# Three quarters of the V sums kept in PSUM, and the experts' stage written as a fixed pipeline in program order

## The chip, the cores and the metric

The kernel runs on 1 core of one Trainium2 chip. The metric is device time in microseconds, the median of several runs of the whole kernel; lower is better. A profile is one such execution with the hardware profiler on. PE is TensorE (PEld its weight loads), DVE is VectorE, ACT is ScalarE, POOL is GpSimd and SP is SyncE, which here issues the ordinary DMAs.

## The reference

One encoder layer on 256 tokens of width 2048 in float32: a retention and a recurrent group in parallel, cross attention over 256 memory tokens, then a feed-forward layer of 16384 one-neuron experts, and a last RMSNorm. The change is in the experts' layer:

```python
def peer_ffn(xn, w_q, sub_keys, u_tab, v_tab):
    q = (xt @ w_q).reshape(t, PEER_HEADS, 2, PEER_HALF)
    sub_scores = jnp.einsum('thcd,hckd->thck', q, sub_keys)
    ...                      # eid: 8 heads x top 16 experts of each token; gate: their softmax
    u = u_tab[eb]
    act = jax.nn.gelu(jnp.einsum('td,tkd->tk', xb, u))
    return jnp.einsum('tk,tkd->td', gb * act, v_tab[eb])
```

## The kernel before

The 16384 experts are split. 104 of 128 columns of them (`RD`) are computed **densely**, for all 256 tokens, in 13 chunks (`NCH`) of 8 columns of 128 experts. The experts of the other 24 columns are **gathered** row by row for the tokens that chose them, and a few that don't fit in the gathers' 28 slots per token tile (`BASE`) go through a short "spill" path.

A dense chunk has two halves. The U half (`u_chunk`, L909) multiplies the tokens by 8 blocks of U: each block is two loads of 512 KB, and each load is one **step** of 8 matmuls with `hi` and 8 with `lo`. The V half (`v_unit`, L935) multiplies the gated activations by V: four column groups `dc` of 512 columns, four steps `q` each, and 12 matmuls per step (two token tiles, two k, three products). So a half chunk is 16 steps either way.

Every step has the same preparation. SP loads 512 KB into one of 4 `raw` buffers (`raw_tile`, L105). `split` (L110) rounds it on ACT to `hi` (L114, 4 buffers) and has DVE subtract to get `lo` (L115, 3 buffers), which frees `raw`. PE then multiplies (U: L124 with `hi`, L127 with `lo`; V: L931 to L933). Every second step of U ends a block: ACT copies a half of the sum (L917), DVE adds it (L918), ACT takes the gelu (L919). After each `dc` group of V, DVE adds the two finished PSUM tiles into the output rows `hh` (L951), 8 times per chunk.

Between the halves stands `prep` (L878): two loads of gate values `gd` into `raw` buffers, two DVE multiplies (L883) and the split of the gated activations into `ah` and `al` (L894, L895; chunks 8 to 11 use a second place, `xe`).

The gathers run beside all this. `chosen` (L991) makes 112 tasks: POOL gathers 128 rows (L964) into a ring of four `gat` buffers, three tasks ahead; DVE then either takes their dot products with the tokens (`dot`, L981, whose product goes to a PSUM tile `junk` that nobody reads) or adds them weighted into `hh` (`axpy`, L989). `weigh` (L975) finds up to 8 weights before a block of dots. A task costs 2.2 credits, a weight 0.225, and every step pays in 0.9 (`RC`, `Weave.pump`), so a task falls to about every 2.4 steps.

The program is written in the order of chunks: six U halves first (`LEAD`), then V of chunk i and U of chunk i+6 in turn until U is done (7 pairs), then V alone (chunks 7 to 11), then `v_final` with chunk 12 and the output. But the order in which each engine gets its instructions is chosen by the Tile framework's scheduler, from priorities and its own idea of times. PSUM before: 4 banks for products (`ps`), 4 for small ones (`ps2`), which `junk` takes over in the experts' stage.

Of the kernel before, what the change touches and what calls it, by code (L numbers as in the profile page):

```python
# [17 lines left out]
P = 128  # L18
# [52 lines left out]
def hybrid_layer_kernel(ctx: ExitStack, tc: tile.TileContext, a: dict, out: bass.AP, dbg=None):  # L71
# [4 lines left out]
    ws = ctx.enter_context(tc.tile_pool(name="ws", bufs=1))  # L76
    b8 = ctx.enter_context(tc.tile_pool(name="b8", bufs=2))
    rp = ctx.enter_context(tc.tile_pool(name="rp", bufs=1))
    ps = ctx.enter_context(tc.tile_pool(name="ps", bufs=4, space=bass.MemoryType.PSUM))
    dp = ctx.enter_context(tc.tile_pool(name="dp", bufs=1, space=bass.MemoryType.DRAM))  # L80
    ps2 = tc.tile_pool(name="ps2", bufs=4, space=bass.MemoryType.PSUM)
    ps2_ = ps2.__enter__()
    wv = Weave()
# [21 lines left out]
    def raw_tile(src):  # L105
        t = ws.tile([P, 1024], F32, tag="raw", name="raw", bufs=4)
        nc.sync.dma_start(t, src)
        return t

    def split(raw, hi=None, lo=None):  # L110
        if hi is None:
            hi = ws.tile([P, 1024], F32R, tag="hi", name="hi", bufs=4)
            lo = ws.tile([P, 1024], F32R, tag="lo", name="lo", bufs=3)
        A.copy(hi, raw)  # L114
        V.tensor_tensor(lo, raw, hi.bitcast(F32), op=ALU.subtract)  # L115
        return hi, lo

    def whalf(j, src, xt, pt, raw=None):
        hi, lo = split(raw_tile(src) if raw is None else raw)
        for part in ((0, 1) if j == 0 else (1, 0)):  # L120
            for k in range(8):
                kb = 8 * j + k
                if part == 0:
                    PE.matmul(pt, hi[:, k * P:(k + 1) * P], xt[:, kb, :],  # L124
                              start=(kb == 0), stop=(kb == KB - 1))
                else:
                    PE.matmul(pt[:, :T], lo[:, k * P:(k + 1) * P], xt[:, kb, :T],  # L127
                              start=False, stop=False)
        wv.pump(wv.rate)

    def wblock(srcs, xt, pt):
# [767 lines left out]
    def tick(n):  # L899
        if wave and n % 3 == 2:  # L900
            if next(wave[0], "end") == "end":
                wave.pop(0)

    def flush():
        while wave:
            for _ in wave.pop(0):
                pass

    def u_chunk(i):  # L909
        act = acts[i] = tp.tile([P, 8, T], F32, tag="act", name=f"act{i}", bufs=LEAD)  # L910
        for c in range(8):
            pt = mm("U")
            for j in range(2):
                whalf(j, a["U"][8 * i + c, j], xn, pt)
                tick(2 * c + j)
            t = tp.tile([P, T], F32, tag="fold", name="foldu", bufs=2)
            A.copy(t, pt[:, T:])  # L917
            V.tensor_tensor(t, pt[:, :T], t, op=ALU.add)  # L918
# [7 lines left out]
    def v_mms(ah, al, hi, lo, q, tt, pt, first=True):  # L926
        t_ = slice(tt * P, (tt + 1) * P)
        for k in range(2):
            c = 2 * q + k
            w = slice(k * 512, (k + 1) * 512)  # L930
            PE.matmul(pt, ah[:, c, t_], hi[:, w], start=(first and c == 0), stop=False)  # L931
            PE.matmul(pt, ah[:, c, t_], lo[:, w], start=False, stop=False)  # L932
            PE.matmul(pt, al[:, c, t_], hi[:, w], start=False, stop=(c == 7))  # L933

    def v_unit(ah, al, i, dc):  # L935
        pts = mm("V0"), mm("V1")
        late = i == SPILL + 2
        if late:
            for tt in range(TT):
                for b in range(OV):  # L940
                    PE.matmul(pts[tt], spl["oh"][:, b, tt * P:(tt + 1) * P],  # L941
                              spl["v"][b][:, dc * 512:(dc + 1) * 512], start=(b == 0), stop=False)
        for q in range(4):
            hi, lo = split(raw_tile(a["V"][i, dc, q]))
            for tt in range(TT):
                v_mms(ah, al, hi, lo, q, tt, pts[tt], not late)
            wv.pump(wv.rate)
            tick(4 * dc + q)
        ds = slice(dc * 512, (dc + 1) * 512)
        for tt in range(TT):  # L950
            V.tensor_tensor(hh[tt][:, ds], hh[tt][:, ds], pts[tt], op=ALU.add)  # L951

    def v_chunk(i):
        ah, al = ahs.pop(i)
        for dc in range(4):
            v_unit(ah, al, i, dc)
            if side:
                next(side[0], None)
        flush()

    def rows(tab, tt, k):
        gat = ring[turn[0] % len(ring)]
# [15 lines left out]
    def dot(tt, k0, n, k, gat):  # L978
        if k == 0:
            dots[tt, k0] = tp.tile([P, 8], F32, tag="dots", name="dots", bufs=2)  # L980
        V.scalar_tensor_tensor(junk, gat, 1.0, h[tt], op0=ALU.mult, op1=ALU.mult,  # L981
                               accum_out=dots[tt, k0][:, k:k + 1])
# [39 lines left out]
    def spill():  # L1022
        od = cp.tile([P, OV], F32, name="od")
        for b in range(OV):
            bs = slice(b, b + 1)
            u, x = fetch("Us", spl["i"][:, bs], "ah"), fetch(None, spl["ti"][:, bs], "al")
            yield
            yield
            V.scalar_tensor_tensor(junk, u, 1.0, x, op0=ALU.mult, op1=ALU.mult, accum_out=od[:, bs])
# [12 lines left out]
        done.add("spill")  # L1042
# [110 lines left out]
    wv.add(chosen(blocks_of(0, 0, BASE) + blocks_of(1, 0, BASE)))  # L1153
    for i in range(NCH - 1):
        both = i + LEAD < NCH
        if i == SPILL:
            side.append(spill())
        if i == SPILL + 2:
            for _ in side.pop():
                pass  # L1160
        if not both:
            wave.append(prep(i + 1))
        v_chunk(i)
        if both:
            wave.append(prep(i + 1))
            u_chunk(i + LEAD)
    wv.drain()
    rest()
    v_final(NCH - 1)
# [92 lines left out]
```

## Time and profile before

| | us |
|---|---|
| median of 3 runs | 2249.35 (2247.98 to 2252.21) |
| the profiled execution | 2251.4 |
| its span, first to last instruction | 2249.6 |
| PE busy | 2162.1 (96%) |
| DVE busy | 1719.4 (76%) |
| ACT busy | 1085.0 (48%) |
| POOL busy | 293.0 (13%) |

Times inside the execution are counted from the span's start. The six U halves begin at about 920 us, the first V product is at 1274.8, V runs alone from about 1950, and `v_final` starts at about 2195. Matmul records overlap, so a PE that is busy all the time is told by its idle gaps, and its speed by the distance from one matmul's start to the next.

### The profile page before, as it was taken

The page shows a single profiled execution, that of the slowest core. Times are in us where ns is not written, and L with a number is a line of the kernel's source. Part 1 is how long each engine was busy: PE and PEld are TensorE (multiplying, and loading weights), DVE is VectorE, ACT ScalarE, POOL GpSimd, SP SyncE. Part 2 cuts the span into 40 slices and gives each one's busy share as a digit, 9 for nine tenths or more (in the row PEclk, how much of TensorE's full clock was granted, in tenths as well). Part 3 has the DMA queues.
Part 4 walks back from the last instruction along what each step waited for, and adds up shares of the span by engine and source line. Part 5 has one row for each costly group of instructions (what it writes and reads, how often), then busy time and mean ns, then how long its engine had stood idle before and what let it go on. Part 6 is the DMA issues. An engine that isn't in the chain of part 4 may idle for free. (4 is left out here: it accounts for less than half of the span.)

```text
span 2249.6 us, 29992 instructions
## 1 busy us (share of the span) xinstructions
PE 2162.1 (96%) x10900; PEld 1815.7 (81%) x10900; DVE 1719.4 (76%) x2458; ACT 1085.0 (48%) x1640; POOL 293.0 (13%) x178
## 2 busy tenths in 40 slices
PE   8999989999999999999999799999999899999998
PEld 6877878888888888888899687878878687877786
DVE  6748876645544569999877799997788898779865
ACT  6564434444544455545789443434434343533344
POOL 0303121000000000000000113211122211124101
PEclk9999999999999999999999899999999999999999
DMA  8664645666644575555765799977797997879664
GB/s 277 235 210 151 211 133 165 187 191 185 185 143 140 170 258 182 175 180 188 254 215 157 266 354 361 330 284 281 259 331 279 346 350 255 306 279 349 218 203 141
DMA packets 157207, 527.82 MB, mean 235 GB/s; under 512 B 17078, under 2 KB 46390, under 8 KB 142902
## 3 DMA queue, kind: packets, MB, share of 16 engines
q1 hardware_dynamic: 139776, 419.36, 56.0%
q0 software_dynamic: 17280, 106.53, 12.5%
q8 instruction: 85, 1.39, 0.3%
q14 instruction: 66, 0.54, 0.1%
HBM read 525.21 MB, written 19.92 MB: 242 GB/s over the span
## 5 line engine op out<-in xcount | busy, mean ns | idle before, releaser
L115 DVE TENSOR_TENSOR lo<-raw,hi 128x1024 fp32r<-128x1024 f32 x700 | 860.7, 1245 | 341.9 <-PE xc L163 140.9
L114 ACT CAST hi<-raw 128x1024 fp32r<-128x1024 f32 x700 | 734.1, 1050 | 744.1 <-PE V L933 167.9
L124 PE MATMUL U<-xn,hi 128*128 128x512 f32 x1664 | 414.8, 397 | 2.2 <-ACT hi L114 2.2
L124 PEld LDWEIGHTS U<-xn,hi 128*128 128x128 f32 x1664 | 308.2, 191 | 61.3 <-ACT hi L114 2.7
L932 PE MATMUL V<-lo,ah 128*128 128x512 f32 x560 | 228.1, 407 | 21.0 <-DVE lo L115 20.6
L127 PE MATMUL U<-xn,lo 128*128 128x256 f32 x1664 | 229.5, 287 | 12.5 <-DVE lo L115 12.5
L127 PEld LDWEIGHTS U<-xn,lo 128*128 128x128 f32 x1664 | 218.4, 193 | 23.8 <-DVE lo L115 15.4
L931 PE MATMUL V<-hi,ah 128*128 128x512 f32 x560 | 224.5, 401 | 1.3 <-ACT hi L114 1.3
L933 PE MATMUL V<-hi,al 128*128 128x512 f32 x560 | 224.2, 400 | 0.0
L964 POOL DMA_INDIRECT gat<-in_Us_dram,idx x56 | 85.2, 1521 | 634.5 <-PE U L127 235.1
L964 POOL DMA_INDIRECT gat<-in_Vs_dram,idx x56 | 107.5, 1919 | 411.7 <-DVE hh L989 348.3
L932 PEld LDWEIGHTS V<-lo,ah 128*128 128x128 f32 x560 | 107.4, 192 | 53.4 <-DVE lo L115 27.7
L981 DVE SCALAR_TENSOR_TENSOR junk<-gat,h 128x2048 f32<-128x2048 f32 x56 | 128.4, 2294 | 20.4 <-DMA gat<-in_Us_dram,idx 20.2
L989 DVE SCALAR_TENSOR_TENSOR hh<-gat,coef,hh 128x2048 f32<-128x2048 f32 x56 | 131.5, 2348 | 2.1 <-DMA gat<-in_Vs_dram,idx 1.6
L931 PEld LDWEIGHTS V<-hi,ah 128*128 128x128 f32 x560 | 107.4, 192 | 28.5 <-ACT hi L114 1.5
L933 PEld LDWEIGHTS V<-hi,al 128*128 128x128 f32 x560 | 107.5, 192 | 25.2
L124 PE MATMUL wb<-hT,hi 128*128 128x512 f32 x448 | 113.9, 398 | 1.0 <-ACT hi L114 1.0
L932 PE MATMUL V<-lo,xe 128*128 128x512 f32 x256 | 101.6, 397 | 7.5 <-DVE lo L115 7.5
L931 PE MATMUL V<-hi,xe 128*128 128x512 f32 x256 | 102.3, 400 | 0.0
L933 PE MATMUL V<-hi,xe 128*128 128x512 f32 x256 | 100.9, 394 | 0.0
L124 PEld LDWEIGHTS wb<-hT,hi 128*128 128x128 f32 x448 | 81.3, 189 | 16.7 <-ACT hi L114 1.2
L124 PE MATMUL wb<-xT,hi 128*128 128x512 f32 x368 | 91.0, 398 | 0.2 <-ACT hi L114 0.2
(381 smaller groups left out, 3290.4 us busy)
## 6 DMA issues: line engine op xcount, KB each, us to landing
raw<-in_U_dram SPq DMA_DIRECT2D x208, 512.0 KB
raw<-in_V_dram SPq DMA_DIRECT2D x208, 512.0 KB
raw<-in_w_xyg_dram SPq DMA_DIRECT2D x48, 512.0 KB
raw<-in_w_qkv_dram SPq DMA_DIRECT2D x48, 512.0 KB
raw<-in_w_xk_dram SPq DMA_DIRECT2D x32, 512.0 KB
raw<-in_w_xv_dram SPq DMA_DIRECT2D x32, 512.0 KB
raw<-in_w_out_dram SPq DMA_DIRECT2D x32, 512.0 KB
raw<-in_w_xq_dram SPq DMA_DIRECT2D x32, 512.0 KB
```

Source lines behind the costliest of these rows:

```text
L114: A.copy(hi, raw)
L115: V.tensor_tensor(lo, raw, hi.bitcast(F32), op=ALU.subtract)
L124: PE.matmul(pt, hi[:, k * P:(k + 1) * P], xt[:, kb, :], start=(kb == 0), stop=(kb == KB - 1))
L127: PE.matmul(pt[:, :T], lo[:, k * P:(k + 1) * P], xt[:, kb, :T], start=False, stop=False)
L931: PE.matmul(pt, ah[:, c, t_], hi[:, w], start=(first and c == 0), stop=False)
L932: PE.matmul(pt, ah[:, c, t_], lo[:, w], start=False, stop=False)
L933: PE.matmul(pt, al[:, c, t_], hi[:, w], start=False, stop=(c == 7))
L964: G.indirect_dma_start(gat, None, a[tab], bass.IndirectOffsetOnAxis(ap=idx[tt][:, k:k + 1], axis=0), bounds_check=NS - 1, oob_is_err=False)
L981: V.scalar_tensor_tensor(junk, gat, 1.0, h[tt], op0=ALU.mult, op1=ALU.mult, accum_out=dots[tt, k0][:, k:k + 1])
L989: V.scalar_tensor_tensor(hh[tt], gat, coef[tt, k0][:, k:k + 1], hh[tt], op0=ALU.mult, op1=ALU.add)
```

## The change

**PSUM.** The 4 product banks are made of two pools of 2, used in turn as one ring of 4, up to the experts' stage. There the second pool and the 4 small banks are given up for six accumulators `acc` (three `dc` groups by two token tiles), in which the V sums of `dc` 0 to 2 stay over all 13 chunks; `v_final` adds them into `hh` once. Only `dc` 3 still uses product banks and is added into `hh` after each chunk. `dot` writes its unread product over the gathered rows, since `junk` is gone. The spill's matmuls come at the end of chunk 10's groups, not at their start.

**Order.** From the first V half to the end of chunk 11, the steps are one list, run by `run` under a manual schedule: every engine gets its instructions in the order in which the program states them. At step t these are, in turn: what an earlier step left for ACT, `hi` of step t+3, `lo` of step t+2, the load of step t+6, the matmuls of step t, what an earlier step left for DVE, and the tasks that the 0.9 credits pay for. A load of gate values is a step of its own without matmuls ("G"): two per chunk, in the U half after its 3rd and 6th steps, or in V alone after the 2nd and 5th. V's groups go 0, 3, 1, 2.

The buffers of `raw`, `hi`, `lo`, `gat` and the task credits are as before, and so is the order of every engine up to the end of the first six U halves, but for three dots that the scheduler had put there and that now come in `run`.

```diff
-    ps = ctx.enter_context(tc.tile_pool(name="ps", bufs=4, space=bass.MemoryType.PSUM))
+    ps = ctx.enter_context(tc.tile_pool(name="ps", bufs=2, space=bass.MemoryType.PSUM))
...
+    psx = tc.tile_pool(name="psx", bufs=2, space=bass.MemoryType.PSUM)
+    banks = [ps, ps, psx.__enter__(), psx]
+    banks[3] = banks[2]
...
+    def v_steps(i):
+        for dc in (0, 3, 1, 2):
+            kept = dc < 3
...
+            def products(hi, lo, q, dc=dc, kept=kept, box=box):
...
+                    box.extend(acc[dc] if kept else (mm("V0"), mm("V1")))
...
+                for tt in range(TT):
+                    v_mms(ah, al, hi, lo, q, tt, box[tt], not kept or i == 0, not kept and not late)
...
+            def added(dc=dc, kept=kept, box=box):
+                if not kept:
+                    ds = slice(dc * 512, (dc + 1) * 512)
+                    for tt in range(TT):
+                        V.tensor_tensor(hh[tt][:, ds], hh[tt][:, ds], box[tt], op=ALU.add)
+                if side:
+                    next(side[0], None)
...
+            for q in range(4):
+                yield (a["V"][i, dc, q], lambda hi, lo, q=q, f=products: f(hi, lo, q),
+                       {1: [(None, added)]} if q == 3 else {})
...
+                    post = {1: [(lambda c=c: halved(c), lambda c=c: summed(c))],
+                            2: [(lambda c=c: curved(c), None)]}
...
+    def prep_steps(i):
...
+                post = {2: [(lambda: rounded(0), None)], 4: [(lambda: rounded(1), lambda: left(0))],
+                        6: [(None, lambda: left(1))]}
+            yield gd[i, :, tt * P:(tt + 1) * P, :].rearrange("p t c -> p (t c)"), lambda g, tt=tt: gate(g, tt), post
...
+    def run(steps):
...
+        for t, step in enumerate(steps):
+            now = later.pop(t, [])
+            for f, _ in now:
+                if f:
+                    f()
+            high(t + 3)
+            low(t + 2)
+            load(t + 6)
+            if step[0] == "W":
+                step[2](his.pop(t), los.pop(t))
+            for _, f in now:
+                if f:
+                    f()
+            for n, fs in step[3].items():
+                later.setdefault(t + n, []).extend(fs)
+            if step[0] == "W":
+                wv.pump(wv.rate)
...
-        V.scalar_tensor_tensor(junk, gat, 1.0, h[tt], op0=ALU.mult, op1=ALU.mult,
+        V.scalar_tensor_tensor(gat, gat, 1.0, h[tt], op0=ALU.mult, op1=ALU.mult,
...
-    junk = pjt.tile([P, D], F32, tag="junk", name="junk")
+    acc = [[pjt.tile([P, 512], F32, name=f"acc{dc}{tt}") for tt in range(TT)] for dc in range(3)]
...
     for i in range(NCH - 1):
...
+        if i + LEAD < NCH:
+            steps += woven(v_steps(i), [], 0, 0)
+            steps += woven(u_steps(i + LEAD), prep_steps(i + 1), 3, 4)
+        else:
+            steps += woven(v_steps(i), prep_steps(i + 1), 2, 4)
...
+    with tc.manual_schedule(engines=ENGINES):
+        run(steps)
```

DVE's queue in the first V half, before. `lo` is the subtraction that PE waits for, `junk` a dot, `hh<-hh,V` the addition of a finished V group.

```order
L115 TENSOR_TENSOR lo<-raw,hi 128x1024 x2
L981 SCALAR_TENSOR_TENSOR junk,dots<-gat_11271,h_4187 128x2048
L115 TENSOR_TENSOR lo<-raw,hi 128x1024
L951 TENSOR_TENSOR hh_11261<-hh_11261,V_11389 128x512
L981 SCALAR_TENSOR_TENSOR junk,dots<-gat_11272,h_4187 128x2048
L951 TENSOR_TENSOR hh_11262<-hh_11262,V_11390 128x512
L115 TENSOR_TENSOR lo<-raw,hi 128x1024 x2
```

The same queue at the same place after the change; L1082 is the `lo` of `run`, L1136 the dot, L991 the one addition that is left.

```order
L1082 TENSOR_TENSOR lo<-raw,hi 128x1024 x2
L1136 SCALAR_TENSOR_TENSOR gat_11275,dots<-gat_11275,h_4190 128x2048
L1082 TENSOR_TENSOR lo<-raw,hi 128x1024 x2
L1136 SCALAR_TENSOR_TENSOR gat_11276,dots<-gat_11276,h_4190 128x2048
L1082 TENSOR_TENSOR lo<-raw,hi 128x1024 x2
L991 TENSOR_TENSOR hh_11264<-hh_11264,V_11424 128x512
L991 TENSOR_TENSOR hh_11265<-hh_11265,V_11425 128x512
L1082 TENSOR_TENSOR lo<-raw,hi 128x1024
L1136 SCALAR_TENSOR_TENSOR gat_11277,dots<-gat_11277,h_4190 128x2048
```

A dot no longer shares its place with additions: it stands alone between two or three subtractions, and three of four pairs of additions are gone.

DVE's queue in the U half of the first pair, before, where the gate values are multiplied in (`act<-raw,act`) and the activations split (`al`); `foldu` ends a U block, `gj` finds a weight, `hh<-gat,coef,hh` is an axpy.

```order
L883 TENSOR_TENSOR act_7951<-raw,act_7951 128x8x128
L951 TENSOR_TENSOR hh_11262<-hh_11262,V_11558 128x512
L115 TENSOR_TENSOR lo<-raw,hi 128x1024
L975 SCALAR_TENSOR_TENSOR gj,gsel<-key,sel,gsp 128x128
L989 SCALAR_TENSOR_TENSOR hh_11261<-gat_11271,coef,hh_11261 128x2048
L115 TENSOR_TENSOR lo<-raw,hi 128x1024
L918 TENSOR_TENSOR foldu<-U,foldu 128x256
```

And after; L1033 is the multiplication, L1141 the product of a block's dots with their weights, which needs ACT's gelu of the dot just ahead of it.

```order
L1033 TENSOR_TENSOR act_7954<-raw,act_7954 128x8x128
L1082 TENSOR_TENSOR lo<-raw,hi 128x1024
L1013 TENSOR_TENSOR foldu<-U,foldu 128x256
L1082 TENSOR_TENSOR lo<-raw,hi 128x1024 x2
L1136 SCALAR_TENSOR_TENSOR gat_11277,dots<-gat_11277,h_4190 128x2048
L1141 TENSOR_TENSOR coef<-coef,gsel 128x8
L1033 TENSOR_TENSOR act_7954<-raw,act_7954 128x8x128
```

The multiplication has moved from the V half's last additions into the U half's steps, with subtractions ahead of and behind it, and L1141 now stands right behind its dot.

PE's queue where the six U halves end and V begins, before.

```order
L127 MATMUL U<-xn,lo 128x256 x8
L931 MATMUL V_11282<-hi,ah 128x512
L931 MATMUL V_11283<-hi,ah 128x512
L127 MATMUL U<-xn,lo 128x256 x8
L124 MATMUL U<-xn,hi 128x512 x8
L932 MATMUL V_11282<-lo,ah 128x512
```

After the change.

```order
L128 MATMUL U<-xn,hi 128x512 x16
L131 MATMUL U<-xn,lo 128x256 x16
L128 MATMUL U<-xn,hi 128x512 x8
L939 MATMUL acc_11285<-hi,ah 128x512
L940 MATMUL acc_11285<-lo,ah 128x512
```

V's first matmuls no longer stand between U's; all of U comes first.

More of the change, by code (lines that the diff above doesn't have):

```diff
@@ L43 @@
 AHEAD = 3
+ENGINES = None
 class Weave:
@@ L116, in split, with w_mms @@
         return hi, lo
-    def whalf(j, src, xt, pt, raw=None):
-        hi, lo = split(raw_tile(src) if raw is None else raw)
+    def w_mms(j, hi, lo, xt, pt):
         for part in ((0, 1) if j == 0 else (1, 0)):
@@ L128, in whalf @@
                               start=False, stop=False)
+    def whalf(j, src, xt, pt, raw=None):
+        hi, lo = split(raw_tile(src) if raw is None else raw)
+        w_mms(j, hi, lo, xt, pt)
         wv.pump(wv.rate)
@@ L924, in u_chunk, with v_mms @@
         flush()
-    def v_mms(ah, al, hi, lo, q, tt, pt, first=True):
+    def v_mms(ah, al, hi, lo, q, tt, pt, first=True, last=True):
         t_ = slice(tt * P, (tt + 1) * P)
@@ L932, in v_mms @@
             PE.matmul(pt, ah[:, c, t_], lo[:, w], start=False, stop=False)
-            PE.matmul(pt, al[:, c, t_], hi[:, w], start=False, stop=(c == 7))
+            PE.matmul(pt, al[:, c, t_], hi[:, w], start=False, stop=(last and c == 7))
     def v_unit(ah, al, i, dc):
-        pts = mm("V0"), mm("V1")
+        kept = dc < 3
+        pts = acc[dc] if kept else (mm("V0"), mm("V1"))
+        first, last = not kept or i == 0, not kept or i == NCH - 1
         late = i == SPILL + 2
+        for q in range(4):
+            hi, lo = split(raw_tile(a["V"][i, dc, q]))
+            for tt in range(TT):
+                v_mms(ah, al, hi, lo, q, tt, pts[tt], first, last and not late)
+            wv.pump(wv.rate)
+            tick(4 * dc + q)
         if late:
@@ L941, in v_unit @@
                     PE.matmul(pts[tt], spl["oh"][:, b, tt * P:(tt + 1) * P],
-                              spl["v"][b][:, dc * 512:(dc + 1) * 512], start=(b == 0), stop=False)
-        for q in range(4):
-            hi, lo = split(raw_tile(a["V"][i, dc, q]))
+                              spl["v"][b][:, dc * 512:(dc + 1) * 512], start=False, stop=(last and b == OV - 1))
+        if last:
+            ds = slice(dc * 512, (dc + 1) * 512)
             for tt in range(TT):
-                v_mms(ah, al, hi, lo, q, tt, pts[tt], not late)
-            wv.pump(wv.rate)
-            tick(4 * dc + q)
@@ new lines, in u_steps, with products, halved, summed @@
+    def u_steps(i):
+        box = {}
+        def products(hi, lo, c, j):
+            if j == 0:
+                box[c] = mm("U")
+            w_mms(j, hi, lo, xn, box[c])
+        def halved(c):
+            box["t", c] = t = tp.tile([P, T], F32, tag="fold", name="foldu", bufs=2)
+            A.copy(t, box[c][:, T:])
+        def summed(c):
+            t = box["t", c]
+            V.tensor_tensor(t, box[c][:, :T], t, op=ALU.add)
+        def curved(c):
+            if c == 0:
+                acts[i] = tp.tile([P, 8, T], F32, tag="act", name=f"act{i}", bufs=LEAD)
+            A.activation(acts[i][:, c, :], box["t", c], AF.Gelu_apprx_tanh)
+        for c in range(8):
+            for j in range(2):
+                post = {}
+                if j == 1:
+                    post = {1: [(lambda c=c: halved(c), lambda c=c: summed(c))],
+                            2: [(lambda c=c: curved(c), None)]}
+                yield a["U"][8 * i + c, j], lambda hi, lo, c=c, j=j: products(hi, lo, c, j), post
@@ new lines, in woven, with load, high, low @@
+    def woven(main, extra, first, apart):
+        main, extra = list(main), list(extra)
+        for n, e in enumerate(extra):
+            main.insert(first + n * apart, ("G",) + e)
+        return [m if m[0] == "G" else ("W",) + m for m in main]
+    def run(steps):
+        raws, his, los, later = {}, {}, {}, {}
+        def load(t):
+            if 0 <= t < len(steps):
+                raws[t] = raw_tile(steps[t][1])
+        def high(t):
+            if 0 <= t < len(steps) and steps[t][0] == "W":
+                his[t] = ws.tile([P, 1024], F32R, tag="hi", name="hi", bufs=4)
+                A.copy(his[t], raws[t])
+        def low(t):
+            if 0 <= t < len(steps):
+                if steps[t][0] == "W":
+                    los[t] = ws.tile([P, 1024], F32R, tag="lo", name="lo", bufs=3)
+                    V.tensor_tensor(los[t], raws[t], his[t].bitcast(F32), op=ALU.subtract)
+                else:
+                    steps[t][2](raws[t])
+                del raws[t]
+        for t in range(4):
+            load(t)
+        for t in range(3):
+            high(t)
+        for t in range(2):
+            low(t)
+            load(t + 4)
+        for t, step in enumerate(steps):
[14 more added lines that the diff above has]
+            if step[0] == "W":
+                wv.pump(wv.rate)
+        for t in sorted(later):
+            for f in [x[0] for x in later[t]] + [x[1] for x in later[t]]:
+                if f:
+                    f()
@@ L1143, in hybrid_layer_kernel @@
     ps2.__exit__(None, None, None)
+    psx.__exit__(None, None, None)
+    banks[:] = [ps]
     pc = tc.tile_pool(name="pc", bufs=1, reuse_waits="tile")
@@ L1150, in hybrid_layer_kernel, with begin, g @@
     pjt = pj.__enter__()
-    junk = pjt.tile([P, D], F32, tag="junk", name="junk")
+    acc = [[pjt.tile([P, 512], F32, name=f"acc{dc}{tt}") for tt in range(TT)] for dc in range(3)]
     wv.rate = RC
     wv.add(chosen(blocks_of(0, 0, BASE) + blocks_of(1, 0, BASE)))
+    steps = []
     for i in range(NCH - 1):
-        both = i + LEAD < NCH
-        if i == SPILL:
-            side.append(spill())
[L1158 to L1166, printed above, removed]
+        if i + LEAD < NCH:
+            steps += woven(v_steps(i), [], 0, 0)
+            steps += woven(u_steps(i + LEAD), prep_steps(i + 1), 3, 4)
+        else:
+            steps += woven(v_steps(i), prep_steps(i + 1), 2, 4)
+        if i == SPILL - 1:
+            mark = len(steps)
+    def begin(f):
+        def g(*x):
+            side.append(spill())
+            f(*x)
+        return g
+    steps[mark] = steps[mark][:2] + (begin(steps[mark][2]),) + steps[mark][3:]
+    with tc.manual_schedule(engines=ENGINES):
+        run(steps)
     wv.drain()
```

54 lines of the change are left out of this document (43 added, 11 removed).

## The prediction

> **What bounds the kernel now.** I read the page's first part, then the busy time by stretch, the waits of PE, and one such wait in order of time.
>
> ```profile
> span 2249.6 us, 29992 instructions
> PE 2162.1 (96%) x10900; PEld 1815.7 (81%) x10900; DVE 1719.4 (76%) x2458; ACT 1085.0 (48%) x1640; POOL 293.0 (13%) x178
> ```
>
> PE is busy nearly always, so a change can only win what PE idles and what it loses in clock. By stretch (length, busy time of PE, PEld, DVE, ACT and POOL, then granted clock, DMA share, GB/s), for the pairs of V and U, for V alone, for both together, and for the end:
>
> ```profile
> core 0: us, PE busy (x) PEld busy (x) DVE busy (x) ACT busy (x) POOL busy (x), PEclk, DMA share, GB/s
> 1279.00:1950.00 671.00, 643.33 (x3138) 535.44 (x3138) 582.37 (x625) 283.46 (x358) 143.39 (x91) 0.98 0.85 312
> 1950.00:2195.00 245.00, 236.89 (x990) 186.97 (x989) 197.95 (x177) 93.69 (x94) 46.99 (x21) 0.99 0.75 259
> 1279.00:2195.00 916.00, 880.22 (x4127) 722.40 (x4127) 780.32 (x801) 377.15 (x451) 190.38 (x112) 0.98 0.83 298
> 2195.00:2250.00 55.00, 45.11 (x192) 35.66 (x191) 31.07 (x45) 23.29 (x36) 9.98 (x6) 0.96 0.43 142
> ```
>
> The changed stage is the third row: PE idles 916 - 880.2 = 35.8 us in it. The waits of PE there (total, times, longest) have one cause:
>
> ```profile
> PE V L932 <- DVE lo L115: 28.1, 19, 4.7
> PE U L127 <- DVE lo L115: 7.1, 6, 2.2
> ```
>
> `lo` comes late. One such wait in order of time:
>
> ```profile
> 1288.14 2.30 DVE L981 SCALAR_TENSOR_TENSOR junk<-gat,h 128x2048 f32<-128x2048 f32 x1 [1.99 <-DMA gat<-in_Us_dram,idx]
> 1290.36 0.35 DVE L975 SCALAR_TENSOR_TENSOR gj<-key,sel,gsp 128x128 f32<-128x128 f32 x1
> 1290.63 1.22 DVE L115 TENSOR_TENSOR lo<-raw,hi 128x1024 fp32r<-128x1024 f32 x1
> 1291.90 0.50 PE L932 MATMUL V<-lo,ah 128*128 128x512 f32 x1 [2.41 <-DVE lo L115]
> 1293.25 0.63 PE L931 MATMUL V<-hi,ah 128*128 128x512 f32 x1
> 1297.54 0.39 PE L931 MATMUL V<-hi,ah 128*128 128x512 f32 x1
> ```
>
> DVE sat 1.99 us on a gather that hadn't landed, did the dot and a weight, and only then the subtraction; PE waited 2.41 us. Soon after, the same matmul takes 0.63 us in place of 0.39: the clock is down for a while. So a wait costs more than its gap.
>
> How long is the stage at full speed? The rows are two undisturbed V matmuls ten places apart, a stretch of V alone, 16 matmuls each of U's `lo` and `hi` on the chain, and the spill's matmuls:
>
> ```profile
> 1704.71 0.40 PE L932 MATMUL V<-lo,ah 128*128 128x512 f32 x1
> 1707.05 0.39 PE L933 MATMUL V<-hi,al 128*128 128x512 f32 x1
> 2150.00:2175.00 25.00, 25.00 (x112) 20.70 (x111) 19.93 (x20) 11.39 (x11) 0.00 (x0) 1.00 0.72 232
> 1709.29 1.91 PE U L127 x16
> 1711.21 3.65 PE U L124 x16
> 2093.86 3.43 PE V L941 x8
> ```
>
> V from `ah`: 2.34/10 = 0.234 us a matmul, 192 of them 44.9 us a half. V from `xe`: 25/110 = 0.227 (two of the 112 lie across the edges), 43.6 us a half. U: (1.91 + 3.65) x 8 = 44.5 us a half. Spill: 4 x 3.43 = 13.7. The stage holds 8, 4 and 7 such halves: 359.2 + 174.4 + 311.5 + 13.7 = 858.8 us. A step is 2.79 us (44.5 to 44.9 over 16). The stage takes 916, so **57.2 us** can be won: 35.8 idle, and 21.4 mostly clock (0.02 x 916 = 18.3).
>
> **The change part by part.** What DVE does in the stage, by group (count, busy, mean ns, idle time before and its causes):
>
> ```profile
> L115 DVE TENSOR_TENSOR lo<-raw,hi 128x1024 fp32r<-128x1024 f32 x306 | 367.8, 1220 | 81.8 <-PE V L932 39.2 <-ACT hi L114 25.4 <-issue 10.8
> L989 DVE SCALAR_TENSOR_TENSOR hh<-gat,coef,hh 128x2048 f32<-128x2048 f32 x56 | 131.5, 2348 | 2.1 <-DMA gat<-in_Vs_dram,idx 1.6
> L981 DVE SCALAR_TENSOR_TENSOR junk<-gat,h 128x2048 f32<-128x2048 f32 x53 | 121.6, 2294 | 20.4 <-DMA gat<-in_Us_dram,idx 20.2
> L951 DVE TENSOR_TENSOR hh<-hh,V 128x512 f32<-128x512 f32 x95 | 64.0, 681 | 4.7 <-PE V L933 4.7
> L883 DVE TENSOR_TENSOR act<-raw,act 128x1024 f32<-128x1024 f32 x24 | 51.6, 2151 | 22.3 <-DMA raw<-gd 22.3
> L918 DVE TENSOR_TENSOR foldu<-U,foldu 128x256 f32<-128x256 f32 x57 | 23.9, 419 | 4.5 <-ACT foldu L917 4.5
> L975 DVE SCALAR_TENSOR_TENSOR gj<-key,sel,gsp 128x128 f32<-128x128 f32 x56 | 19.5, 349 | 0.5
> L895 DVE TENSOR_TENSOR al<-act,ah 128x1024 fp32r<-128x1024 f32 x16 | 19.5, 1222 | 0.0
> ```
>
> *PSUM.* 24 additions of `dc` 3 stay (12 chunks, two tiles), 71 go: 71 x 0.681 = 48.4 us less of DVE. Three dots come in (3 x 2.29 = 6.9), and 56 dots now write to where the axpys write: between no change and 56 x (2.348 - 2.294) = 3.0; I take 3.0. DVE falls from 780.3 to 742 us. None of this is on PE's path by itself; its worth is that `lo` waits behind less. The last additions (six, in `v_final`) are the ones that stood there already, and the spill's matmuls only change places.
>
> *Order.* DVE no longer stops on a transfer, or briefly. A gather is issued three tasks ahead, 3 x 2.4 steps x 2.79 us = 20 us, against
>
> ```profile
> DMA to landing us min/median/max: 4.5/7.9/13.5
> ```
>
> so the 20.2 us of waiting go; the gate values are loaded as far ahead as any step, and of their 22.3 us little stays. One wait is added: L1141 stands right behind its dot and needs ACT's gelu of it. Behind it on DVE stands a `lo`, for which PE waits. ACT's next row may be held up by a load, so it costs between nothing and some 3 us, 8 times; the lead below hides it.
>
> *The lead.* `lo` of step t+2 is started when step t starts (its buffer comes free then), so it has 2 x 2.79 - 1.22 = 4.4 us to spare, and a dot of 2.3 ahead of it fits. What DVE has per half, with tasks at 14.4 credits of 259 in all (112 x 2.2 + 56 x 0.225) for 56 x (2.294 + 2.348 + 0.349) = 279.5 us, 15.5 us a half: V 16 x 1.22 + 2 x 0.68 + 15.5 = 36.4 against PE's 44.9; U 19.5 + 8 x 0.42 + 2 x 2.15 + 2 x 1.22 + 15.5 = 45.1 against 44.5; V alone 19.5 + 1.4 + 6.7 + 15.5 = 43.1 against 43.6. Rows overlap (the dot at 1288.14 lasts 2.30, yet the next row starts 2.22 later), so these are a few per cent too high. DVE fits everywhere, in U and in V alone with next to no room.
>
> *The loads.* ACT's part of a step:
>
> ```profile
> L114 ACT CAST hi<-raw 128x1024 fp32r<-128x1024 f32 x305 | 320.1, 1051 | 444.9 <-DMA raw<-in_V_dram 159.8 <-PE V L933 158.1 <-DMA raw<-in_U_dram 108.2
> ```
>
> A `raw` buffer is taken for a load's landing, 1.05 us of `hi`, 1.22 of `lo` and DVE's queue. Four buffers must turn in 4 x 2.79 = 11.2 us, so a load may take 8.9 us, or 6.5 with a dot in front; PE stops only 4.4 later. Loads on the chain, from issue to landing:
>
> ```profile
> 1485.24 8.71 DMA raw<-in_V_dram
> 1532.38 5.92 DMA raw<-in_U_dram
> 1744.54 12.28 DMA raw<-in_V_dram
> ```
>
> These are near the limit. How PE fares at a given load is read from a calm stretch and two tight ones:
>
> ```profile
> 1545.00:1635.00 90.00, 90.00 (x450) 75.81 (x450) 66.69 (x61) 40.77 (x51) 8.93 (x6) 1.00 0.75 264
> 1815.00:1860.00 45.00, 43.69 (x243) 37.70 (x242) 41.57 (x39) 23.21 (x33) 9.04 (x7) 1.00 0.92 334
> 1365.00:1410.00 45.00, 41.44 (x181) 33.26 (x180) 40.29 (x49) 17.85 (x22) 11.96 (x8) 0.96 0.96 370
> ```
>
> With DMA at 0.75 PE loses nothing; at 0.92 it loses 1.3 of 45 us, 2.9%; at 0.96, 3.6 us and 4% of clock, 12%. A stage of about 877 us moves the same bytes, evenly: 0.83 x 916/877 = 0.87. That is 70% of the way from 0.75 to 0.92: 2.0% of 858.8, **17.5 us** still lost (bounds 0 and 12%). So 57.2 - 17.5 = 39.7 go.
>
> *The start.* Before V begins, PE waits on a `lo` behind two dots:
>
> ```profile
> 1257.03 2.29 DVE L981 SCALAR_TENSOR_TENSOR junk<-gat,h 128x2048 f32<-128x2048 f32 x1
> 1264.81 3.78 PE L127 MATMUL U<-xn,lo 128*128 128x256 f32 x16 [3.52 <-DVE lo L115]
> ```
>
> Those leave; a memset of a gather buffer takes part of their place, and V's first sums now wait for banks that U's last block may hold (0 to 0.8 us, a copy and an addition). Between 0 and 3.5 us are won; I take 1.
>
> Sum: 2251.4 - 39.7 - 1 = 2210.7 for the profiled execution, which lies 2.05 above the median of 2249.35; for the median, **2209**.
>
> [...]
>
> **The rivals.**
>
> 1. *The loads pace U and the gated V halves.* These have 18 loads in a half, not 16. At a landing of 7.3 us (mean of the first two chain rows) and half a dot of queue, a buffer turns in 7.3 + 2.27 + 1.17 = 10.7 us, and 18/4 turns take 48.3 us against 44.5: 3.8 lost in each of 11 halves, 42 in all; V's 16 loads take 43, under its 44.9. Won: 57.2 - 42 + 1 = 16, **2233**. For it: DVE idled 25.4 us for `hi`, and U has no room on DVE. Against: the calm stretch holds U steps at full speed.
> 2. *Nearly nothing stays lost* (under 1%): evenly spread gathers never make the loads late. Won 49 to 58, **2192 to 2200**. Against it: DVE's 43 to 45 us in two kinds of half.
> 3. *The clock's share stays*, being due to something else than gaps. Then 35.8 x 0.69 (the part won above) + 1 = 26 go: **2223**. Against it: 0.63 us rows right behind the gap, and a clock of 1.00 in the calm stretch. [...]
> 4. *Slower.* With a gather in flight at every step, all loads land late, and no engine may go past its place in the order. The 304 steps of 19 halves and 24 gate loads are 82 turns of the four buffers; above 916/82 = 11.2 us a turn the stage is longer than now, that is from a mean landing of 7.7 us with half a dot. At 8.2: 82 x 11.64 = 954, **2287**. For it: 8.71 and 12.28 above. Against: those rows stand on the chain because they were late, and 334 GB/s went with 2.9% lost.
> 5. *No change*: bytes, not their order, set the pace: within 0.2%, 4.5 us, about what a measurement here can tell from nothing. That the change doesn't do what it says is out: the queues show the new order.
>
> **How the numbers follow.** Forecast (1 to 3% still lost, 2200 to 2218) 0.45; rivals 1 to 5: 0.24, 0.11, 0.07, 0.08, 0.05. The time is the forecast's, 2209. The range 2196 to 2236 holds the forecast, the first and third rival and part of the second. Faster: 0.45 + 0.24 + 0.11 + 0.07 = 0.87; same 0.05; slower 0.08.
>
> **What would show it.** Right: PE's waits for `lo` in the stage fall from 35 us to about 10, the clock rises to 0.99, additions into `hh` from 95 to 24, DVE's waits for gathers and gate values from 42 us to a few, DMA 0.87. First rival: gaps gather in the U halves, with ACT waiting for loads. Wrong: PE idles as now, or `lo` waits for `hi` through most of the stage.

## The result, and the profile after

The changed kernel takes 2212.45 us (median of 4 runs, 2209.82 to 2217.56) against 2250.78 for the kernel before (4 runs, one more than in the table above): a ratio of 0.983, interval 0.981 to 0.986. The forecast was 2209, with a range of 2196 to 2236. The profiled execution took 2212.09 us at a mean granted clock of 0.99 (before 2251.4 at 0.982). Its first lines:

```profile
span 2210.3 us, 29998 instructions
PE 2142.8 (97%) x10900; PEld 1805.8 (82%) x10900; DVE 1682.8 (76%) x2386; ACT 1084.3 (49%) x1640; POOL 307.0 (14%) x178
```

The busy time by stretch of the kernel after, in the columns of the forecast: the seven pairs, V alone, both together, and the end.

```profile
1274.60:1907.00 632.40, 626.45 (x3134) 527.34 (x3135) 544.95 (x564) 279.79 (x354) 155.70 (x86) 1.00 0.88 325
1907.00:2156.00 249.00, 238.84 (x998) 188.44 (x997) 198.39 (x170) 95.46 (x96) 57.44 (x28) 0.99 0.78 276
1274.60:2156.00 881.40, 865.29 (x4130) 715.78 (x4131) 743.34 (x733) 375.26 (x450) 213.15 (x114) 1.00 0.85 311
2156.00:2210.00 54.00, 45.09 (x195) 35.91 (x193) 30.76 (x44) 23.44 (x36) 9.91 (x6) 0.97 0.45 145
```

The stage fell from 916 to 881.4 us and begins 4.4 us earlier (1274.6 against 1279; by then the kernel before had begun five matmuls of V, and from the same matmul to the same it is 3.1). All of the stage's gain came from the pairs, 671 to 632.4. V alone, 245 us before, takes 249. PE's idle time in the stage fell from 35.8 to 16.1 us. Its waits there (total, times, longest):

```profile
PE acc L940 <- DVE lo L1082: 5.4, 3, 4.8
PE U L131 <- DVE lo L1082: 4.4, 3, 1.6
PE V L940 <- DVE lo L1082: 3.4, 2, 2.6
PE U L128 <- DVE foldu L1013: 1.5, 1, 1.5
PE acc L939 <- DVE foldu L926: 1.1, 1, 1.1
```

Where 25 waits for `lo` cost 35.2 us, 8 cost 13.2. The last two rows are waits for banks, of a kind that the kernel before doesn't have. What DVE waits for in the stage, the largest causes and the new one:

```profile
DVE lo L1082 <- issue: 44.2, 42, 4.7
DVE lo L1082 <- ACT hi L1076: 42.0, 40, 2.8
DVE act L1033 <- DMA raw<-gd: 2.9, 3, 1.4
DVE coef L1141 <- ACT coef L1140: 2.2, 8, 0.3
```

No row names a gather any more, where 20.2 us stood; of 22.3 us of waits for gate values 2.9 are left. The added wait, L1141, costs 0.3 us eight times. DVE's groups:

```profile
L1136 DVE SCALAR_TENSOR_TENSOR gat<-gat,h 128x2048 f32<-128x2048 f32 x56 | 127.9, 2284 | 0.0
L991 DVE TENSOR_TENSOR hh<-hh,V 128x512 f32<-128x512 f32 x24 | 15.4, 680 | 0.6 <-PE V L983 0.6
L1184 DVE SCALAR_TENSOR_TENSOR spl<-spl 128x2048 f32<-128x2048 f32 x2 | 4.6, 2278 | 0.0
```

24 additions are left of 95. The longest wait of PE that remains, 4.77 us at 1991.28, has this on DVE ahead of it, in order of time:

```profile
1983.25 1.22 DVE L1051 TENSOR_TENSOR xe<-act,xe 128x1024 fp32r<-128x1024 f32 x1
1984.39 1.27 DVE L991 TENSOR_TENSOR hh<-hh,V 128x512 f32<-128x512 f32 x2
1985.59 2.28 DVE L1184 SCALAR_TENSOR_TENSOR spl<-spl 128x2048 f32<-128x2048 f32 x1
1987.80 2.28 DVE L1136 SCALAR_TENSOR_TENSOR gat<-gat,h 128x2048 f32<-128x2048 f32 x1
1990.01 1.22 DVE L1082 TENSOR_TENSOR lo<-raw,hi 128x1024 fp32r<-128x1024 f32 x1
```

A split, two additions, the spill's dot and a task's dot, 6.8 us, stand ahead of one `lo`: more than the 4.4 us of lead. Right behind that wait the clock is at half speed for 3.4 us:

```profile
1985.00:1991.20 6.20, 1.51 (x7) 0.93 (x5) 6.20 (x8) 2.24 (x3) 0.84 (x1) 1.00 0.27 106
1991.20:1994.60 3.40, 3.32 (x8) 2.65 (x9) 3.40 (x5) 0.00 (x0) 2.85 (x2) 0.50 0.63 213
```

One other such stretch is left in the stage, at 2025.3 (3.4 us at a clock of 0.51), behind a wait of 2.60 us on a `lo` with the second spill dot and an axpy ahead of it.

### The profile page after: what moved, and what is told of

It reads as the page before. It is cut to its first block, busy times and chain, and to the rows that moved or that the text cites. A ratio compares the mean times of both kernels' runs of the same rounds, so it can differ in the third digit from the quotient of the medians.

```text
span 2210.3 us, 29998 instructions
## 1 busy us (share of the span) xinstructions
PE 2142.8 (97%) x10900; PEld 1805.8 (82%) x10900; DVE 1682.8 (76%) x2386; ACT 1084.3 (49%) x1640; POOL 307.0 (14%) x178
## 3 DMA queue, kind: packets, MB, share of 16 engines
q0 software_dynamic: 17280, 106.53, 12.3%
## 4 chain that ended last, share of the span: by engine, by line
PE 80%; DVE 10%; DMA 4%; ACT 2%; issue 2%; POOL 0%; DVEq 0%; ACTq 0%; SPq 0%; POOLq 0%
PE U L128 15%; PE U L131 8%; PE acc L940 6%; PE acc L939 6%; PE acc L941 6%; PE wb L128 6%; PE xc L171 6%; PE xc L172 6%; PE xc L170 6%; PE wb L131 3%; DVE lo L120 3%; PE G L873 2%; PE V L940 2%; PE V L941 2%; PE V L939 2%
## 5 line engine op out<-in xcount | busy, mean ns | idle before, releaser
L1082 DVE TENSOR_TENSOR lo<-raw,hi 128x1024 fp32r<-128x1024 f32 x304 | 368.7, 1221 | 127.3 <-issue 44.2
L1119 POOL DMA_INDIRECT gat<-in_Us_dram,idx x56 | 97.0, 1731 | 727.8 <-DVE gat L1136 279.1
L939 PE MATMUL acc<-hi,ah 128*128 128x512 f32 x432 | 171.0, 396 | 1.1 <-DVE foldu L926 1.1
L940 PE MATMUL acc<-lo,ah 128*128 128x512 f32 x432 | 171.5, 397 | 0.0
L941 PE MATMUL acc<-hi,al 128*128 128x512 f32 x432 | 169.6, 393 | 0.0
L1136 DVE SCALAR_TENSOR_TENSOR gat<-gat,h 128x2048 f32<-128x2048 f32 x56 | 127.9, 2284 | 0.0
L939 PEld LDWEIGHTS acc<-hi,ah 128*128 128x128 f32 x432 | 81.1, 188 | 21.8 <-DVE foldu L926 1.5
L941 PEld LDWEIGHTS acc<-hi,al 128*128 128x128 f32 x432 | 81.1, 188 | 19.7
L940 PEld LDWEIGHTS acc<-lo,ah 128*128 128x128 f32 x432 | 81.1, 188 | 19.0
L863 ACT ACTIVATE o<-o,trio 128x104 f32<-128x104 f32 x256 | 75.6, 371 | 12.2 <-DVE o L860 11.6
```

Of the source, the lines that this page charges most:

```text
L941: PE.matmul(pt, al[:, c, t_], hi[:, w], start=False, stop=(last and c == 7))
L1082: V.tensor_tensor(los[t], raws[t], his[t].bitcast(F32), op=ALU.subtract)
L1119: G.indirect_dma_start(gat, None, a[tab], bass.IndirectOffsetOnAxis(ap=idx[tt][:, k:k + 1], axis=0), bounds_check=NS - 1, oob_is_err=False)
```

## The experiments

The theory: in the scheduler's order DVE stops on gathers and gate values with a `lo` behind it (42.5 us of waits in the stage before, 20.2 and 22.3), and the fixed order ends that. The main rival: the 71 additions that went are what counts (below, "kept" sums are those that stay in PSUM over all chunks). A second question is what the 22.6 us are that the stage still takes over full speed (881.4 - 858.8). Times are medians, ratios are against the kernel before on the same chip.

**The order without the kept sums.** In `v_steps` and `v_unit`:

```
-            kept = dc < 3
+            kept = False
...
-                    box.extend(acc[dc] if kept else (mm("V0"), mm("V1")))
+                    box.extend(acc[dc] if dc < 3 else (mm("V0"), mm("V1")))
```

> The fixed pipeline stays, but every V half adds all its sums into hh again (six more additions a half, 72 in the stage, 72 x 0.681 = 49 us more of DVE); the six banks are kept and started anew each chunk. Theory (the gain is the order: `lo` keeps its lead whatever DVE's load, as long as DVE fits): DVE in a V half is 36.4 + 4.1 = 40.5 us against PE's 44.9 and in V alone 43.1 + 4.1 = 47.2 against 43.6, so the pairs stay and V alone gives back up to 4 x 3.6 = 14 us: 2212 to 2228, most of the 38 us kept. Rival (the gain is the 71 additions that went): 2240 to 2252.

2223.93 us, ratio 0.989 (0.987 to 0.991). The stage of this kernel, in the columns of the busy time by stretch, and its group of additions:

```profile
1274.60:2167.30 892.70, 872.12 (x4131) 716.51 (x4131) 784.34 (x804) 374.84 (x449) 212.85 (x114) 0.99 0.84 307
```

```profile
L991 DVE TENSOR_TENSOR hh<-hh,acc 128x512 f32<-128x512 f32 x71 | 45.7, 682 | 4.8 <-PE acc L983 3.9 <-PE acc L941 0.9
```

DVE is busier than in the kernel before (784.3 us against 780.3), and the stage is 23.3 us shorter than 916. So the order (with the banks and the dots' new place, which the run "the banks alone" below finds to be worth nothing by themselves) brings some 27 of the 38 us, and on top of it the kept sums bring 11.5, a quarter of the 48 us of DVE work that they remove. That is the theory's case.

**The kept sums without the order.** The loop of before, calling the changed `v_unit`:

```
+    def v_chunk(i):
+        ah, al = ahs.pop(i)
+        for dc in range(4):
+            v_unit(ah, al, i, dc)
+            if side:
+                next(side[0], None)
+        flush()
...
-    with tc.manual_schedule(engines=ENGINES):
-        run(steps)
...
+        v_chunk(i)
...
```

> The three quarters of V's sums stay in PSUM and the dots write in place, but the stage runs through the loop of before, in the order that the scheduler gives. Theory (the order): DVE still stops at gathers and gate values (about 42 us) and PE waits about 30 us for `lo`; the 48 us of DVE that go shorten few of these waits: 2236 to 2250. Rival (the additions): 2208 to 2220.

2269.16 us, ratio 1.008 (1.006 to 1.011): slower than before, which neither had expected. Waits of PE and of DVE in this kernel's stage:

```profile
PE U L128 <- DVE hh L962: 22.1, 7, 8.4
PE acc L940 <- DVE lo L120: 16.9, 15, 2.6
```

```profile
DVE act L891 <- DMA raw<-gd: 33.5, 14, 5.4
DVE gat L1144 <- DMA gat<-in_Us_dram,idx: 30.8, 19, 3.3
DVE hh L1152 <- DMA gat<-in_Vs_dram,idx: 13.8, 7, 4.4
```

DVE waits 78.1 us for transfers. The largest wait of PE is new: U's first matmul needs a bank, and the two that are left both hold V's last quarter, not yet added. My next theory was that these two banks are the trouble.

**The list of steps without its order.** The kernel after, with the queues filled by the scheduler:

```
-    with tc.manual_schedule(engines=ENGINES):
-        run(steps)
+    run(steps)
```

> The kernel after with its own list of steps, but the queues are filled by the scheduler and not in the order of the program. Theory (what wins is that nothing is moved ahead of a `lo` that is due): the scheduler moves dots, weights and gate products ahead as in before, waits of PE for `lo` return to 20 us or more: 2230 to 2250. Rival 1 (the list of steps itself, with loads six ahead and gates spread over the steps, is enough): 2208 to 2218. Rival 2 (the additions): the same 2208 to 2218.

2275.28 us, ratio 1.012 (1.010 to 1.015), beyond every value given. DVE in its stage:

```profile
DVE gat L1136 <- DMA gat<-in_Us_dram,idx: 31.2, 17, 3.6
DVE hh L1144 <- DMA gat<-in_Vs_dram,idx: 30.3, 15, 4.3
DVE act L1033 <- DMA raw<-gd: 28.7, 12, 5.1
```

90.2 us of waits for transfers, with PE's for `lo` back at 42.3 us. The same steps, loads and banks cost 63 us more when the scheduler orders them. This is the cleanest sign that the order is what counts.

**The bank taken out of U's way.** The kept sums in the scheduler's order, but quarter 3 second:

```
-        for dc in range(4):
+        for dc in (0, 3, 1, 2):
```

> As the kernel with the sums kept in PSUM and the loop of before, but with V's quarters in the order 0, 3, 1, 2, so that the quarter that is added (dc 3) lies in the middle of the half, and U's first block finds its bank empty. Theory (in the order 0, 1, 2, 3 what made it slower than before was that only two banks are left for U and dc 3: 22.1 us of PE waiting for the addition of dc 3, 3.3 for foldu): 2269 less 25, and some clock: 2238 to 2246, so that the additions alone bring 5 to 12 us against before. Rival (the kept sums hurt elsewhere): 2260 or more.

2278.09 us, ratio 1.012 (1.009 to 1.016). The wait of U for the addition is gone, and waits for `lo` (42.1 us in the stage) and for U's fold (12.3) stand in its place. The theory of the bank fell.

**The banks alone.** The scheduler's order, the banks of after, all sums added (`kept = False` as above, with the loop of before):

> The loop of before with all sums added in every half as before, but with the banks of after (six banks that only V's first three quarters use, two for U and dc 3): against the run with the sums kept it tells what keeping is worth in the old order, against before what the banks cost. Theory 1 (two banks for U and dc 3 make the slowness; the 72 additions that go still save something): 2275 to 2295, slower than the kept version's 2269. Theory 2 (banks cost, and the removed additions only let DVE arrive sooner at transfers that it then waits for): 2263 to 2274. Rival (the banks cost nothing, and keeping the sums is what hurts): 2244 to 2256, as before.

2249.98 us, ratio 1.000 (0.998 to 1.001). The rival was right: the banks cost nothing in the whole time, and in the scheduler's order it is the kept sums that hurt, by 19 us. In its profiled execution (2238.74, 11 under its median), two waits of DVE and two of its groups:

```profile
DVE act L891 <- DMA raw<-gd: 27.1, 12, 5.9
DVE gat L1144 <- DMA gat<-in_Us_dram,idx: 18.3, 12, 5.1
```

```profile
L1152 DVE SCALAR_TENSOR_TENSOR hh<-gat,coef,hh 128x2048 f32<-128x2048 f32 x56 | 131.5, 2349 | 0.6
L962 DVE TENSOR_TENSOR hh<-hh,acc 128x512 f32<-128x512 f32 x72 | 48.8, 684 | 8.4 <-PE acc L941 4.9 <-PE acc L957 3.4
```

DVE waits 45.4 us for gathers and gate values (the axpys at most 0.6 more). With the 72 additions gone (48.8 us) it waited 78.1, some 32 more: two thirds of the removed work came back as waiting. One place in the kernel with kept sums shows how:

```profile
1690.46 2.29 DVE L1144 SCALAR_TENSOR_TENSOR gat<-gat,h 128x2048 f32<-128x2048 f32 x1 [1.26 <-DMA gat<-in_Us_dram,idx]
1692.67 1.22 DVE L120 TENSOR_TENSOR lo<-raw,hi 128x1024 fp32r<-128x1024 f32 x1
1695.80 2.29 DVE L1144 SCALAR_TENSOR_TENSOR gat<-gat,h 128x2048 f32<-128x2048 f32 x1 [1.91 <-DMA gat<-in_Us_dram,idx]
1705.96 2.29 DVE L1144 SCALAR_TENSOR_TENSOR gat<-gat,h 128x2048 f32<-128x2048 f32 x1 [2.07 <-DMA gat<-in_Us_dram,idx]
```

Three of four dots there wait 1.3 to 2.1 us for a gather (the fourth, at 1700.45, doesn't), and every `lo` behind them waits too. Why PE lost 19 us more, and not just no less, isn't settled. In the two profiles its waits for a bank grow most, from 9.2 us (8.7 for an addition, 0.5 for a fold) to 25.4, and those for `lo` from 22.3 to 29.2; but with the bank out of U's way the time was no better. The scheduler orders the two kernels differently, and no run held its order fixed while the additions went.

**The spill's dots counted as tasks**, so that no task follows them at once:

```
             V.scalar_tensor_tensor(u, u, 1.0, x, op0=ALU.mult, op1=ALU.mult, accum_out=od[:, bs])
+            wv.credit -= 2.2
```

> The kernel after, but each of the spill's two dots counts 2.2 against the allowance of DVE tasks, so that no dot or axpy is put right behind it. Theory (what is still lost in V alone is `lo` late behind two long instructions, 4.77 and 2.60 us with their neighbours, and the half-speed clock of 3.4 us behind each): these two gaps and both half-clock stretches go, 7.4 + 3.4 = 8 to 11 us: 2201 to 2205. Rival (these gaps are late loads that show up there): they move on, 2210 to 2214.

2208.44 us, ratio 0.982 (0.979 to 0.984). The waits of PE in V alone, which were 10.2 us in the kernel after, are:

```profile
PE acc L940 <- DVE lo L1082: 4.0, 3, 1.8
PE V L940 <- DVE lo L1082: 1.9, 3, 0.8
```

The two long waits are gone, and smaller ones came in their place: three that I put down to late loads, one of 1.66 us behind a split, two additions and the spill's dot, and one of 1.76 us, with a half-speed stretch behind it (a clock of 0.71 and 0.79 over the next two 3.4 us), where a late `hi`, a split, two additions and the spill's last small instructions come together. 4 us won where 8 to 11 were expected, between the two ranges, and the interval doesn't part it from the kernel after: half right at best.

**No gathers**: `rows` returns its buffer without the indirect DMA.

> The kernel after without its 112 gathers of 1 MB (the dots and axpys run on what lies in the buffers, so that the output lacks those experts); all of DVE's work and its order stay. Theory (what is still lost, 22.6 us over full speed, is late loads behind the gathers, in U halves with gate values and in V alone): the stage comes within some 5 us of full speed, 2190 to 2198. Rival (it is DVE's queue, two long instructions in a row): as after, 2206 to 2213.

2197.51 us, ratio 0.976 (0.974 to 0.979), with the stage at:

```profile
1272.70:2140.00 867.30, 860.79 (x4130) 713.82 (x4131) 742.78 (x733) 374.60 (x450) 14.48 (x6) 1.00 0.66 208
```

DVE does the same work in the same order, and of the 22.6 us over full speed 8.5 are left. So some 14 us of what is still lost goes with the gathers' load on the transfers (DMA's share falls from 0.85 to 0.66); all else, DVE's queue by itself among it, makes less than half.

**Both bursts on DVE taken apart**: the spill as above, and each weight ahead of its own dot.

```
+                if f is dot:
+                    weigh_one(tt, k0, k)
                 f(tt, k0, n, k, held[m - AHEAD])
-                yield 2.2
+                yield 2.425 if f is dot else 2.2
```

> The kernel after with both bursts on DVE taken apart: the spill's dots count 2.2 against the allowance of tasks, and each of the 56 weights stands ahead of its own dot and not eight in a row ahead of the first. Theory (late loads make the rest): of the gaps only the one of 1.60 us behind eight weights goes, 2204 to 2209, as with the spill's dots alone (2208). Rival (bursts on DVE): 2197 to 2203.

2213.62 us, ratio 0.984 (0.981 to 0.987): nothing won, and above both ranges. Even the gap of 1.60 us that stood behind eight weights is there (1.57): a late load, for whose `hi` DVE stands 1.26 us, and a dot of 2.29 us stand in their place.

**Gate loads eight steps apart, and 0.87 of a task a step**, with both bursts apart:

```
-RA, RB, RC = 1.1, 1.9, 0.9
+RA, RB, RC = 1.1, 1.9, 0.87
...
-            steps += woven(u_steps(i + LEAD), prep_steps(i + 1), 3, 4)
+            steps += woven(u_steps(i + LEAD), prep_steps(i + 1), 3, 8)
         else:
-            steps += woven(v_steps(i), prep_steps(i + 1), 2, 4)
+            steps += woven(v_steps(i), prep_steps(i + 1), 2, 8)
```

> As the kernel with both bursts on DVE taken apart, and besides the allowance of tasks is 0.87 a step in place of 0.9 (gathers a little further apart) and the two gate loads of a half stand eight steps apart and not four. Theory (loads come late where gathers and gate loads bunch): 2196 to 2204. Rival (the mean load on DMA sets it, not its spacing): 2204 to 2210.

2204.48 us, ratio 0.979 (0.977 to 0.982), on the border of the two. PE's waits speak for the theory. Of the kernel after, a late load of the chain and the wait behind it, in a U half:

```profile
1602.12 8.41 DMA raw<-in_U_dram
```

```profile
1612.96 1.22 PE L131 MATMUL U<-xn,lo 128*128 128x256 f32 x8 [1.62 <-DVE lo L1082]
```

A landing of 8.41 us is over the 6.5 that the forecast allowed with a long instruction in front. From 1319 to 1907 the kernel after has 5.9 us of waits, all in U halves, and the version with both bursts apart 6.1 in its U halves. With the loads apart there is one row, and none in a U half:

```profile
PE acc L940 <- DVE lo L1082: 0.5, 2, 0.4
```

The run changed two things, the place of the gate loads and the pace of the gathers; no run parts them.

**And the spill's product four steps behind its gelu**, where DVE had stood 4.5 us on ACT, which stood 6.8 us on a late load, in the last version's profile:

```
         A.activation(od, od, AF.Gelu_apprx_tanh)
+        yield
         V.tensor_tensor(od, od, spl["g"], op=ALU.mult)
```

> As the version with 0.87 of a task a step, gate loads eight apart and both bursts taken apart, and besides the spill's product (the line behind ACT's gelu) comes four steps later, so that DVE doesn't wait there for ACT, which stood 6.8 us on a late load. Theory (the gap of 5.33 us and the half-speed clock behind it, 1.7, come from that wait): 7 us less than 2204: 2196 to 2200. Rival (the late loads of that place stop PE anyway): 2202 to 2207.

2204.04 us, ratio 0.979 (0.977 to 0.982): the gap of 5.33 us is gone from the profile, the median is the same. The execution that showed the gap took 2209.83 us, 5 above its version's median, so the gap need not have stood in the others. These last two are the quickest versions that compute the whole layer, some 8 us under the kernel after; their intervals still overlap its own a little.

**`lo` one step later in the program**: `low(t + 1)` for `low(t + 2)`, and `load(t + 5)` for `load(t + 6)`.

> The kernel after with `lo` and loads one step later in the order: `lo` of step t+1 when step t starts, so that its lead is 2.79 - 1.22 = 1.6 us and not 4.4. Theory (the gain comes from a lead that covers one long instruction): each of 112 tasks of 2.28 to 2.34 us overruns it by 0.7, 24 gate products of 2.14 by 0.5: 78 + 13 = 91 us of gaps, below the length that brings the clock down: 2270 to 2310. Rival (the order of the queues is enough, whatever the lead): 2212 to 2225.

2220.02 us, ratio 0.987 (0.985 to 0.990). The rival's value, but the edit didn't do what I had meant: 23 of the `lo` still stand on DVE until PE is done with an earlier one (34.9 us in all; 23 and 32.8 us in the kernel after). There the buffers set the start of the `lo`, wherever the program wrote it, and only the places of other instructions against it moved.

**Two `lo` buffers in turn**, in the same order:

```
+        two = [ws.tile([P, 1024], F32R, tag="lo", name="lo", bufs=3) for _ in range(2)]
...
-                    los[t] = ws.tile([P, 1024], F32R, tag="lo", name="lo", bufs=3)
+                    los[t] = two[turns[0] % 2]
+                    turns[0] += 1
```

> As the version with `lo` one step later in the order (2220), but the stage uses two `lo` buffers in turn and not three. The run with the later order showed that DVE runs ahead of the order written, as far as the buffers of `lo` let it; here it can start `lo` of step t+1 only when PE is done with step t-1. Theory (the lead is set by the buffers of `lo`: 2 x 2.79 - 1.22 = 4.4 us with three, 2.79 - 1.22 = 1.6 with two): each of 112 tasks of 2.28 to 2.34 us overruns it by 0.7, 24 gate products of 2.14 by 0.5: up to 91 us of gaps of under 1 us, 2285 to 2315. Rival (the lead doesn't matter, only the order of the queue and late loads): 2218 to 2232.

2245.43 us, ratio 0.997 (0.995 to 0.998). Waits of PE in the stage:

```profile
PE U L131 <- DVE lo L1085: 14.7, 15, 2.2
PE acc L940 <- DVE lo L1085: 10.6, 6, 3.4
PE V L940 <- DVE lo L1085: 6.3, 6, 3.6
```

The third buffer, which the kernel before has too, is worth 25 us without a change of order, as much as two thirds of what the change won. The sum of 91 us was wrong all the same: a task that stands ahead of a `lo` runs while that `lo` would be waiting for its buffer anyway, so a dot of 2.28 us ends 1.22 + 2.28 - 2.79 = 0.7 us behind the buffer's release, and the `lo` is still done 2.79 - 0.7 - 1.22 = 0.9 us ahead of PE. Only a late load on top, or a second instruction, makes a gap: of the 11 waits of 1 us or more for `lo` in this profile, 8 have two instructions of over 2 us ahead of that `lo` with at most a fold of 0.4 us between them (a gate product or the spill's dot, and a task).

## Why the prediction was right, step by step

*What can be won.* 57.2 us of the stage were put up for winning. 34.6 went there (916 - 881.4), 22.6 stayed.

*Order.* Right: gathers 20.2 to no row, gate values 22.3 to 2.9, and the fixed order without the kept sums wins 27 of 38 us, while the scheduler's order over the same steps loses all of it. The added wait L1141 was put at 0 to 3 us eight times, hidden; it is 0.3.

*PSUM.* The terms were right: 24 additions are left, DVE falls from 780.3 to 743 us (742 forecast). For the dots I took 3.0 us more; they went from 2.294 to 2.284 us. "None of this is on PE's path by itself" holds for the scheduler's order, where the time came back as waits, and beyond: it was slower. On the fixed order the same additions are worth 11.5 us.

*The lead.* The 4.4 us come from three buffers of `lo`, and they are needed: with two, 25 us are lost. That U has "next to no room" on DVE was too dark: the version with the gate loads eight apart has no wait of PE in its U halves.

*The loads.* This is the step that failed, though its sum came near: 17.5 us still lost against 22.6. I read the loss off DMA's share, 2.0% at 0.87. At 0.88 the pairs lost 632.4 - 7 x (44.9 + 44.5) = 6.6 us, 1%; at 0.78 V alone lost 249 - 233 = 16, 7%. So the loss doesn't go by the share. It goes by bunches: two gate loads four steps apart between the gathers, or the spill's dots and gathers. The two waits behind the spill's dots (4.77 and 2.60 us) and the half-speed stretches at them (2 x 1.7) make 10.8 of the 16 us, and the sum had no term for them. With the gate loads eight apart and the gathers a little rarer the U halves lose nothing, at a share of 0.89 as in the kernel after (both from 1319.5 to 1907.7).

*The start* was to win 1 us (0 to 3.5). The 4.4 us between the two stages' starts are 3.1 from the same matmul to the same (1277.7 against 1274.6), and the banks that U's last block holds cost 1.1. One execution of each doesn't fix the size: versions with the program of after up to there begin the stage anywhere from 1274.6 to 1279.5. 34.6 + 4.4 against 39.7 + 1: the forecast's two errors are of opposite sign, and that its total came nearer than its terms is luck.

*The rivals.* The first (loads pace the U halves, 3.8 us lost in each) named the right place with too high a price: the seven U halves lose 1.4 to 2.2 us in four of them, and none with the loads apart (44.6 us each), so 18 loads fit in a half: by the rival's own sum the mean landing is then at most 44.6/4.5 - 2.27 - 1.17 = 6.5 us, and not the 7.3 of two rows of the chain. The second (under 1% lost) and the fifth are out too: 22.6 of 858.8 us is 2.6%. The third, that the clock's share stays, is out: the clock went from 0.98 to 1.00 in the stage as the gaps went. The fourth, slower because all loads land late in the fixed order, didn't come; the versions that were slower are ones whose queues the scheduler fills.

*The clock.* In the stage of the two profiles, before and after, all ten waits of PE of 1.89 us or more have a half-speed stretch at their end, 3.4 us long and once 6.8, with a clock of 0.50 to 0.51; it starts between 0.6 us ahead of the end of the wait and 1.2 us behind. None of the eleven waits of 1.0 to 1.72 us has one, and between the stretches the clock is at 1.00. The length of a wait doesn't decide it alone: with the spill's dots counted as tasks such a stretch follows a wait of 1.76 us, and without gathers none follows one of 2.3 us (the clock is at 1.00 from 1907 to 2140). What else decides it was not shown.

## What to carry to other kernels

Count what stands in an engine's queue ahead of the instruction that the bottleneck waits for (here 6.8 us of DVE's work ahead of one `lo`, and 4.77 us of waiting on PE), before counting how busy the engine is: removing 49 us of DVE's work made this kernel slower in one order and quicker in another. Where transfers are mixed into such a queue, the waits can take the place of the work that is removed (here they went from 45.4 to 78.1 us as 48.8 us of additions went), so change the order first and the work second. What was left after that came in bunches here: spacing loads and gathers further apart took the waits out of the U halves with hardly a change in the bytes moved (326 GB/s against 327).

## What the runs showed that was not expected

Less work on DVE was slower: 48.8 us of additions taken out of the scheduler's order cost 19 us (2249.98 to 2269.16). Where the program writes a `lo` hardly matters (2212 to 2220), how many buffers it has does (2220 to 2245). A dot that overwrites its own input in SBUF (128x2048) took 2.284 us, and one that writes to PSUM 2.294. A half-speed stretch of 3.4 us followed a wait of PE of 1.76 us in one run, and none followed one of 2.3 us in another.
